# Hybrid RWKV-7 / latent-attention layer: eight places for the masked blocks of the recurrence, and raw weights in shared room

## The chip, the cores and the metric

One core of a Trainium2 chip. The core has TensorE (PE, matrix products; the profile shows its weight loads apart as PEld), VectorE (DVE), ScalarE (ACT), GpSimd (POOL) and SyncE (SP). Most transfers are issued from SP's queue, some from POOL's and ACT's; each of these queues is served in order. SBUF holds the working data (128 partitions), PSUM the results of TensorE. The metric is the device time of one execution in microseconds (us).

## The reference

One decoder layer on 2048 tokens of width 1024, in float32. Cut to what matters here:

```python
u = rmsnorm(h, g_pre); proj = u @ w_in           # one input projection for everything
# branch A, RWKV-7, 8 heads x 64: token shift, then per token and head
sa = S @ -kk_t
S  = S * w_t + sa (kk_t * a_t)^T + v_t k_t^T      # the state S is 64 x 64
y_t = S @ r_t                                    # then group norm, bonus, SiLU gate, w_out_a
# branch B: latent attention with rotary keys, SiLU gate, w_out_b
merged = sigmoid(gates_a) * y_a + sigmoid(gates_b) * y_b
h = h + rmsnorm(merged @ w_o, g_post)
```

## The kernel before

Products that need float32 accuracy are made from a high and a low part: `split` casts the high part on ACT and subtracts for the low part on POOL or DVE, and `mm3` makes three products per pair.

The kernel has three stages. The first holds the input projections, the elementwise work of branch A, the recurrence and the gate projections; the second is attention; the third is the output. The change touches the first stage, and names of room in the second.

**Projections.** `proj_seg(s)` works on one of four segments of 512 tokens. `make_xT` normalises the four tiles of x (ACT squares a tile into a scratch output `xjunk`, DVE scales it) and TensorE transposes them into X. Then 17 tiles of 128 columns are projected. `load_w` brings a tile's weights in two halves: a raw half (tag `wraw`, two places) is loaded and split into `whl` (three places); some split tiles are stored and later read back with no split. About half the tiles of segment 0 aren't stored, and are loaded raw again in segment 1. `shift` mixes each result with that of the token before: ACT's product `mf` (two places), DVE's sum in `fsh` (two places), which is then stored. At the start the two small raw weights of the low-rank projections (`lraw`) use the tag `fsh` too.

**The recurrence.** A half segment is 256 tokens, four chunks of 64; there are eight half segments (k = 0 to 7).
- `elem(k)` makes its decays and scaled keys (tiles AR, BK).
- `zblock(k, c)` makes the products of chunk c for all heads, masks them on DVE into a place of Zr, and stores the small diagonal blocks.
- `gather` reads those back, `invert` inverts 32 x 32 blocks with 60 small DVE steps, and `merge` joins them to 64 x 64 inverses.
- `chunk(k, c)` uses a place of Zr, the inverse and the state; it writes the next state (DVE, tile `uv`) and adds to the outputs Y in PSUM.
- `gnorm(k)` normalises the outputs: DVE reads Y's room through transposes `ypt`, which use the same PSUM banks as Y, adds the bonus that was stored in d_ya and stores the sum, four times, through `bvb` (two places).

Zr has six places: place (4k + c) mod 6. `step(k)` issues the chunks of half segment k - 1 among the blocks of half segment k, with `elem(k + 1)`:

```python
zblock(k, E, 0); zblock(k, E, 1)
chunk(k - 1, Ep, 0, ...);  zblock(k, E, 2)
chunk(k - 1, Ep, 1, ...);  zblock(k, E, 3);  gather(k, E)
chunk(k - 1, Ep, 2, ...);  chunk(k - 1, Ep, 3, ...)
# then invert(k), tokmaj(k), gnorm(k - 1), elem(k + 1) in turns, and merge(k)
```

**Order.** The program text gives priorities. A planner walks through it with a model of times, and each engine and queue takes the first instruction in the text that is ready in that model and has room for its tile. The order on each engine is fixed when the kernel is built. Some products (`pin`, `alternate`) keep the order of the text among themselves. Tiles with the same tag share its places; a new tile waits until one is given back.

Of the kernel before, what the change touches and what calls it, by code (L numbers as in the profile page):

```python
# [19 lines left out]
P = 128  # L20
# [29 lines left out]
def hybrid_layer(ctx, tc, x, positions, g_pre, w_in, b_gate, mu_shift, w0, w_decay_up, a0, w_iclr_up, k_k, k_a,  # L50
# [156 lines left out]
    def make_xT(pool, psp, ptag, pbufs, s, g_rep, Xs):  # L207

        XH, XL = Xs
        for i in range(4):  # L210
            tt = s * 4 + i
            if tt < len(x0):
                xt = x0[tt]
            else:
                xt = pool.tile([P, D], F32, name="xt", tag="xt", bufs=2)
                nc.sync.dma_start(xt, x[tt * P:(tt + 1) * P, :])
            junk = pool.tile([P, D], BF16, name="xjunk", tag="xjunk", bufs=1)
            ss = pool.tile([P, 1], F32, name="xss", tag="xss", bufs=2)
            rstd = pool.tile([P, 1], F32, name="xrs", tag="xrs", bufs=2)
            A.activation(junk, xt, AF.Square, accum_out=ss)  # L220
            if s:
                G.tensor_scalar(ss, ss, 1.0 / D, EPS, op0=ALU.mult, op1=ALU.add)
                G.tensor_tensor(rstd, ss, mhalf[:, 0:1], op=ALU.pow)
            else:
                V.tensor_scalar(ss, ss, 1.0 / D, EPS, op0=ALU.mult, op1=ALU.add)
                A.activation(ss, ss, AF.Sqrt)
                V.reciprocal(rstd, ss)
            V.scalar_tensor_tensor(xt, xt, rstd, g_rep, op0=ALU.mult, op1=ALU.mult)
            for k in range(2):
                pt = psp.tile([P, 512], F32, name="xps", tag=ptag, bufs=pbufs)  # L230
                for c in range(4):
                    PE.transpose(pt[:, c * P:(c + 1) * P], xt[:, (4 * k + c) * P:(4 * k + c + 1) * P], ident)
                pv = pt.rearrange("p (c t) -> p c t", c=4)
                hi = XH[:, 4 * k:4 * k + 4, i * P:(i + 1) * P]
                A.copy(hi, pv)
                V.tensor_tensor(XL[:, 4 * k:4 * k + 4, i * P:(i + 1) * P], pv, f32(hi), op=ALU.subtract)
        if s < NS - 1:
            for k in range(4):
                nc.sync.dma_start(d_x[s, k], f32(Xs[k // 2][:, k % 2 * 4:k % 2 * 4 + 4, :]))
# [10 lines left out]

    d_w = {}

    def load_w(pool, src, nk, n, elo=None, bufs=3, tag="w", pieces=None, raws=2, key=None, keep=True):


        res = []
        kept = d_w.get(key)
        if key is not None and kept is None and keep:
            d_w[key] = dtile(f"d_w{key}", [P, -(-nk // 4), 2, 4, n])
        for k0 in range(0, nk, 4):  # L260
            m = min(4, nk - k0)
            w = pool.tile([P, 2, m, P], F32R, name=f"{tag}hl", tag=f"{tag}hl", bufs=bufs)
            wn = w if n == P else w[:, :, :, 0:n]
            if kept is not None:
                nc.sync.dma_start(f32(wn), kept[:, k0 // 4])
            else:
                raw = pool.tile([P, m, P], F32, name=f"{tag}raw", tag=f"{tag}raw", bufs=raws)
                for lo_, n_, ap in (pieces or [(0, n, src)]):
                    nc.sync.dma_start(raw[:, :, lo_:lo_ + n_],
                                      ap[k0 * P:(k0 + m) * P, :].rearrange("(c p) n -> p c n", p=P))  # L270
                split(wn[:, 0], wn[:, 1], raw[:, :, 0:n], A, elo or G)
                if key is not None and keep:
                    nc.sync.dma_start(d_w[key][:, k0 // 4], f32(wn))
            res += [(w[:, 0, c, 0:n], w[:, 1, c, 0:n]) for c in range(m)]
        return res
# [26 lines left out]
    with st:  # L302
# [16 lines left out]
        Xinv = [sb.tile([P, 16, HD], F32, name=f"Xinv{i}") for i in range(2)]  # L319
        for i in range(2):  # L320
            G.memset(Xinv[i], 0.0)
        NZ = 6
        Zr = sb.tile([P, NZ, 2, NP, P], F32, name="Zr")

        def shift(ps, j):

# [6 lines left out]
            return f  # L333

        def wtile(c0, n=P, elo=None, keep=True):
            return load_w(sa, w_in[:, c0:c0 + n], KC, n, elo, key=f"i{c0}", keep=keep)

        def pj():
            return ppa.tile([P, 512], F32, name="pj", tag="pj", bufs=2)
# [89 lines left out]
        def proj_seg(s):  # L429
# [7 lines left out]
                return bool(s or i % 2)  # L437


            ps = pj()  # L440
            proj(ps, wtile(1536, elo=G if s else V, keep=later(0)), X, 2)
            f = shift(ps, 12)
# [17 lines left out]
            for p in range(NP):  # L460
                for nm, c0, j in (("r", 0, 0), ("v", 1024, 8)):
# [6 lines left out]
            ps = pj()  # L468
            k1 = w_in[:, C_KPE:C_KPE + 32]
            proj(ps[0:HD, :], load_w(sa, None, KC, HD, pieces=[(0, 32, k1), (32, 16, k1[:, 16:32]),  # L470
                                                               (48, 16, k1[:, 0:16])], key="kpe"), X)
            rt = sa.tile([P, 512], F32, name="rtab", tag="mf", bufs=2)
            nc.sync.dma_start(rt[0:HD], d_rope[32:96, cols_])
            ra = sa.tile([P, 512], F32, name="ra", tag="fsh", bufs=2)
# [10 lines left out]
        def gates_seg():  # L485

            xs = NS - 1
            for s, i in d_zg:
                if s != xs:
                    xs = s  # L490
                    load_xT(X, s)
                ps = pj()
                c0 = (C_ZA, C_ZB, C_G, C_G + 4 * P, C_G + 8 * P, C_G + 12 * P)[i // 4] + (i % 4) * P
                proj(ps, wtile(c0), X)
                th = sa.tile([P, 512], F32, name="thg", tag="mf", bufs=2)
                if i < 8:
                    A.activation(th, ps, AF.Tanh, scale=0.5)
                    V.scalar_tensor_tensor(th, th, 1.0, ps, op0=ALU.add, op1=ALU.mult)
                else:
                    A.activation(th, ps, AF.Tanh, scale=0.5, bias=dcol(HBG, i - 8))  # L500
                nc.sync.dma_start(d_zg[s, i], th)
                yield
# [4 lines left out]
        def elem(hs, E):  # L507
# [55 lines left out]
            def bonus(e2, p, rf):  # L563

                PE.matmul(e2, lhsT=blk1, rhs=rf, start=True, stop=True)

                def rest():
                    bv = se.tile([P, 256], F32, name="bv", tag="bv", bufs=2)
                    V.tensor_tensor(bv, e2, E["vf"][p], op=ALU.mult)
                    G.tensor_scalar(bv, bv, col("gb", p), None, op0=ALU.add)  # L570
                    nc.sync.dma_start(d_ya[p, s][:, cs_], bv)

                return rest
# [218 lines left out]
        def gnorm(hs, E):  # L792
# [18 lines left out]
                for p in range(NP):  # L811
                    PE.transpose(pts[p // 2][:, p % 2, i, :], y[:, p].rearrange("p h d -> p (h d)"), ident)
            for p in range(NP):
                bv = sb.tile([P, 256], F32, name="bvb", tag="bvb", bufs=2)
                nc.sync.dma_start(bv, d_ya[p, s][:, o:o + 256])
                V.scalar_tensor_tensor(bv, pts[p // 2][:, p % 2].rearrange("p i t -> p (i t)"), col("gg", p),
                                       bv, op0=ALU.mult, op1=ALU.add)
                nc.sync.dma_start(d_ya[p, s][:, o:o + 256], bv)
# [12 lines left out]
        def step(k):  # L831
# [3 lines left out]
                uvq[0] = uv_new() if k < NH else None  # L835
            el = elem(k + 1, new_E(k + 1)) if k + 1 < NH else iter(())
            if E:
                zblock(k, E, 0)
                zblock(k, E, 1)
            if Ep:  # L840
                chunk(k - 1, Ep, 0, Ep["uv"][1])
            if E:
                zblock(k, E, 2)
            yield
            if Ep:
                chunk(k - 1, Ep, 1, Ep["uv"][2])
            if E:
                zblock(k, E, 3)
                gather(k, E)
            next(el, None)  # L850
            yield
            if Ep:
# [20 lines left out]

        ropes = [rope_tables]
        run(proj_seg(0))
        run(elem(0, new_E(0)))
        for s in range(1, NS):
            for k in (0,) if s == 1 else (2 * s - 3, 2 * s - 2):
# [29 lines left out]
        wv3 = w_ukv.rearrange("k (h n) -> k h n", n=P)  # L908
        kws, qws = {}, {}

        def attn_weights(p, pool, bufs):

            kraw = pool.tile([P, 2, P], F32, name="kraw", tag="wqraw", bufs=1)[:, :, 0:HD]
            nc.sync.dma_start(kraw, wv3[:, 2 * p:2 * p + 2, 0:HD])
            kwh = pool.tile([P, P], F32R, name="kwh", tag="kwh", bufs=1)
            kwl = pool.tile([P, P], F32R, name="kwl", tag="kwl", bufs=1)
            split(kwh.rearrange("p (h n) -> p h n", h=2), kwl.rearrange("p (h n) -> p h n", h=2), kraw, A, V)

            kws[p], qws[p] = (kwh, kwl), []
            hq = [w_uq[:, (2 * p + h) * 96:(2 * p + h + 1) * 96] for h in range(2)]  # L920
            for pieces in ([(HD * h, HD, hq[h][:, 0:HD]) for h in range(2)],
                           [x for h in range(2) for x in ((32 * h, 32, hq[h][:, 64:96]),
                                                          (HD + 32 * h, 16, hq[h][:, 80:96]),
                                                          (HD + 32 * h + 16, 16, hq[h][:, 64:80]))]):
                qws[p].append(load_w(pool, None, 2, P, bufs=bufs, tag="wq", pieces=pieces, raws=1))

        tmp = sb.tile([P, NP, 4, P], F32R, name="vtmp", tag="AR", bufs=2).rearrange("p q c t -> p q (c t)")
        vh, vl = tmp[:, 0], tmp[:, 1]
# [1 line left out]
        nc.sync.dma_start(vraw.rearrange("p (h n) -> p h n", n=HD), wv3[:, :, HD:P])  # L930
        split(vh, vl, vraw, A, V)
        sw = kst.enter_context(tc.tile_pool(name="pw", bufs=1, reuse_waits="tile", side="right"))
        attn_weights(0, sw, 2)
        run(step(NH))

        def value(t):
# [62 lines left out]
        def queries(i, Q, sb, psp, ptag, pbufs, cqt=None, rt=None, mm=PE.matmul):  # L999

            p, g = divmod(i, NS)
            if g == 0:
                if p:
                    attn_weights(p, sb, 2)
                yield from keys(p, psp, ptag, pbufs, mm)
            if cqt is None:
                cqt = load_cq(g, sb)
# [419 lines left out]
```

## Time and profile before

| | us |
|---|---|
| median of 3 runs (lowest, highest) | 2454.78 (2450.98, 2462.46) |
| the profiled execution | 2459.4 |
| its span, first to last instruction | 2457.7 |
| TensorE busy in the span | 2216.5 |
| VectorE, ScalarE, GpSimd busy | 1099.8, 710.4, 1020.3 |

Busy time is the time in which at least one instruction of the engine ran. A row of a stretch has the start and the duration in us, the engine (SPq is SP's queue), the line, the operation, the tile written and those read, the shape, how many instructions of the kind stand in the row, and in brackets how long the engine had been idle before it and what ended that.

### The profile page before, as it was taken

What the parts mean: (1) busy time and instruction counts of PE and PEld (TensorE: products, weight loads), DVE (VectorE), ACT (ScalarE), POOL (GpSimd) and SP (SyncE); (2) the same over time, 40 slices, a digit from 0 to 9 for tenths busy, and PEclk for the clock granted to TensorE, in tenths of its full rate; (3) what the DMA queues carried; (4) which work ended last, traced back from release to release, by engine and by line L of the source; (5) the groups of instructions that cost most, each with busy time, mean ns of one, the idle gap of its engine ahead of it and who ended that gap; (6) DMA issues with size and microseconds to landing.
All of it is one profiled execution on the core that took longest, in us unless ns stands there. A gap on an engine that the chain in (4) does not pass through costs nothing.

```text
span 2457.7 us, 37858 instructions
## 1 busy us (share of the span) xinstructions
PE 2216.5 (90%) x14313; PEld 1646.5 (67%) x14313; DVE 1099.8 (45%) x2007; ACT 710.4 (29%) x1283; POOL 1020.3 (42%) x1194
## 2 busy tenths in 40 slices
PE   7978988988989897998698998988999989999997
PEld 5656776767766675776465655555678867788876
DVE  7155675667475847434353435344230231300312
ACT  4343342333324342123233333332321211111111
POOL 6474443445254655222245653555533232312422
PEclk9989989989999998999699999999999999999999
DMA  7777866647657787574211112050297895766863
GB/s 252 217 251 236 242 211 185 191 125 222 178 174 230 233 239 239 170 230 128 72 58 57 49 59 76 29 189 7 82 371 232 282 325 197 283 204 199 318 245 120
DMA packets 315182, 455.15 MB, mean 185 GB/s; under 512 B 114044, under 2 KB 207288, under 8 KB 309368
## 3 DMA queue, kind: packets, MB, share of 16 engines
q1 hardware_dynamic: 285112, 406.06, 51.3%
q0 software_dynamic: 12608, 42.47, 5.2%
q10 hardware_dynamic: 17280, 4.20, 1.0%
q8 instruction: 113, 1.85, 0.3%
q14 instruction: 69, 0.57, 0.1%
HBM read 313.69 MB, written 132.64 MB: 182 GB/s over the span
## 4 chain that ended last, share of the span: by engine, by line
PE 54%; DMA 18%; DVE 17%; POOL 3%; issue 3%; ACT 2%; SPq 2%; ACTq 0%; DVEq 0%; POOLq 0%
PE pj L281 7%; PE pst L294 7%; PE pj L282 7%; PE pj L283 7%; PE po L294 5%; DMA wraw<-in_w_in_dram 3%; DMA whl<-d_wi 3%; DVE mx L1049 3%; DMA Xg<-d_q 2%; DVE Xg L698 2%; DVE tq L696 2%; PE py L281 2%; PE py L283 2%; PE py L282 2%; PE pq L294 2%
## 5 line engine op out<-in xcount | busy, mean ns | idle before, releaser
L281 PE MATMUL pj<-xh,whl 128*128 128x512 f32 (+1 forms) x1320 | 536.4, 406 | 46.3 <-DMA whl<-d_wi 27.1
L283 PE MATMUL pj<-xh,whl 128*128 128x512 f32 (+1 forms) x1320 | 531.9, 403 | 10.0 <-POOL whl L248 9.7
L282 PE MATMUL pj<-xl,whl 128*128 128x512 f32 (+1 forms) x1320 | 529.9, 401 | 0.0
L1172 POOL TENSOR_TENSOR acc<-acc,pt 128x1024 f32<-128x1024 f32 (+2 forms) x144 | 290.5, 2017 | 204.7 <-PE po L294 177.4
L281 PEld LDWEIGHTS pj<-xh,whl 128*128 128x128 f32 x1320 | 256.2, 194 | 116.6 <-DMA whl<-d_wi 29.6
L283 PEld LDWEIGHTS pj<-xh,whl 128*128 128x128 f32 x1320 | 256.1, 194 | 74.1 <-POOL whl L248 15.3
L282 PEld LDWEIGHTS pj<-xl,whl 128*128 128x128 f32 x1320 | 256.4, 194 | 55.6 <-issue 2.5
L1049 DVE TENSOR_REDUCE mx<-pm 128x2 f32<-128x1024 f32 (+3 forms) x160 | 164.4, 1060 | 148.1 <-PE pm L294 147.4
L248 POOL TENSOR_TENSOR whl<-wraw,whl 128x512 fp32r<-128x512 f32 (+1 forms) x114 | 147.4, 1294 | 160.9 <-ACT whl L247 155.8
L1352 DVE SCALAR_TENSOR_TENSOR tg<-tg,py 128x512 f32<-128x512 f32 x64 | 43.9, 687 | 306.0 <-PE py L283 207.1
L1159 ACT ACTIVATE pt<-pst 128x1024 f32<-128x1024 f32 (+2 forms) x144 | 125.2, 883 | 163.5 <-PE pst L294 150.4
L1354 POOL TENSOR_TENSOR tg<-tg 128x512 f32<-128x512 f32 x32 | 41.2, 1288 | 211.7 <-DVE tg L1352 211.7
L247 ACT CAST whl<-wraw 128x512 fp32r<-128x512 f32 (+1 forms) x116 | 71.1, 615 | 179.4 <-DMA wraw<-in_w_in_dram 106.1
L294 PE MATMUL po<-pt,Vt 128*64 128x512 f32 (+3 forms) x576 | 121.4, 538 | 0.0
L281 PE MATMUL py<-BH,whl 128*128 128x512 f32 x256 | 103.2, 404 | 10.2 <-DMA whl<-d_wo 5.2
L294 PE MATMUL pm<-KH,QH 64*128 64x512 f32 (+3 forms) x312 | 71.6, 447 | 40.5 <-DVE mx L1049 34.8
L282 PE MATMUL py<-BL,whl 128*128 128x512 f32 x256 | 102.8, 402 | 0.0
L283 PE MATMUL py<-BH,whl 128*128 128x512 f32 x256 | 102.6, 402 | 0.0
L696 DVE TENSOR_TENSOR tq<-Xg,Qg 128x30 f32<-128x30 f32 (+7 forms) x240 | 84.8, 353 | 38.4 <-DMA Xg<-d_q 33.0
L282 PE MATMUL pout<-wf,MH 128*128 128x512 f32 x256 | 101.1, 395 | 0.0
L283 PE MATMUL pout<-wf,ML 128*128 128x512 f32 x256 | 99.5, 395 | 0.0
L281 PE MATMUL pout<-wf,MH 128*128 128x512 f32 x256 | 97.3, 395 | 0.1
(368 smaller groups left out, 3953.1 us busy)
## 6 DMA issues: line engine op xcount, KB each, us to landing
whl<-d_wi SPq DMA_DIRECT2D x222, 512.0 KB
d_wi<-whl SPq DMA_DIRECT2D x80, 512.0 KB
wraw<-in_w_in_dram SPq DMA_DIRECT2D x98, 256.0 KB
whl<-d_wo SPq DMA_DIRECT2D x48, 512.0 KB
wf<-d_wf SPq DMA_DIRECT2D x48, 512.0 KB
cqt<-d_cq POOLq DMA_DIRECT2D x16, 1024.0 KB, 5.5
d_zg<-thg SPq DMA_DIRECT2D x42, 256.0 KB
xl<-d_x POOLq DMA_DIRECT2D x8, 1024.0 KB, 9.9
```

The lines of the kernel that those rows point to most:

```text
L247: (ehi.copy if ehi is A else ehi.tensor_copy)(hi, src)
L248: elo.tensor_tensor(lo, src, f32(hi), op=ALU.subtract)
L281: mm(ps, lhsT=lh, rhs=rh, start=(i == 0), stop=False)
L282: mm(ps, lhsT=lh, rhs=rl, start=False, stop=False)
L283: mm(ps, lhsT=ll, rhs=rh, start=False, stop=(stop and i == n - 1))
L294: tc.keep_in_program_order(PE.matmul(*args, **kw))
L696: V.tensor_tensor(t3, Xg[:, 0:m, s_:s_ + 1].to_broadcast([P, m, n]), Qg[:, s_:s_ + 1, s_ + 1:32].to_broadcast([P, m, n]), op=ALU.mult)
L698: V.tensor_tensor(Xg[:, 0:m, s_ + 1:32], Xg[:, 0:m, s_ + 1:32], t3, op=ALU.add)
L1049: V.tensor_reduce(mx[:, :, j, c], pm[:, :, 0:w], axis=AX.X, op=ALU.max)
L1159: A.activation(pt[:, :, q0:512], pst[:, :, q0:512], AF.Exp, scale=scale)
L1172: G.tensor_tensor(acc[:, :, q0:512], acc[:, :, q0:512], pt[:, :, q0:512], op=ALU.add)
L1352: V.scalar_tensor_tensor(tg, tg, 1.0, po, op0=ALU.add, op1=ALU.mult)
```

## The change

Zr gets eight places, so that the blocks of two half segments fit; the four blocks of a half segment and its gather are issued ahead of the first chunk of the one before. In segment 0 the raw weights are loaded into the room that Zr takes afterwards (16 places); in the later segments they share `mf`, and in the gate projections `xt`. The scratch output of the Square shares `fsh`; `bv` and `bvb` have one place each; attention's raw weights share `bs`.

```diff
-            junk = pool.tile([P, D], BF16, name="xjunk", tag="xjunk", bufs=1)
+            junk = pool.tile([P, D], BF16, name="xjunk", tag="fsh", bufs=2)
...
-                raw = pool.tile([P, m, P], F32, name=f"{tag}raw", tag=f"{tag}raw", bufs=raws)
+                raw = raw_of(w) if raw_of else pool.tile([P, m, P], F32, name=f"{tag}raw", tag=f"{tag}raw", bufs=raws)
...
-        NZ = 6
-        Zr = sb.tile([P, NZ, 2, NP, P], F32, name="Zr")
+        NZ = 8
+        zraw = sb.tile([P, 4 * NZ // 2, 4, P], F32, name="zraw", tag="Zr", bufs=1)
+        nraw = [0]
+        def raw_first(w):
+            nraw[0] += 1
+            return zraw[:, nraw[0] % (4 * NZ // 2)]
+        def raw_gate(w):
+            return sa.tile([P, 2, 4, P], F32, name="graw", tag="xt", bufs=2)[:, 0]
+        def raw_here(w):
+            return sa.tile([P, 4, P], F32, name="wraw", tag="mf", bufs=2)
...
+            raw_of[0] = raw_here if s else raw_first
...
-                    bv = se.tile([P, 256], F32, name="bv", tag="bv", bufs=2)
+                    bv = se.tile([P, 256], F32, name="bv", tag="bv", bufs=1)
...
-                bv = sb.tile([P, 256], F32, name="bvb", tag="bvb", bufs=2)
+                bv = sb.tile([P, 256], F32, name="bvb", tag="bvb", bufs=1)
...
             if E:
-                zblock(k, E, 0)
-                zblock(k, E, 1)
+                for c in range(4):
+                    zblock(k, E, c)
+                gather(k, E)
             if Ep:
                 chunk(k - 1, Ep, 0, Ep["uv"][1])
-            if E:
-                zblock(k, E, 2)
             yield
             if Ep:
                 chunk(k - 1, Ep, 1, Ep["uv"][2])
-            if E:
-                zblock(k, E, 3)
-                gather(k, E)
...
         run(proj_seg(0))
+        Zr = sb.tile([P, NZ, 2, NP, P], F32, name="Zr", tag="Zr", bufs=1)
         run(elem(0, new_E(0)))
...
+            def raw_of(w):
+                return rpool.tile([P, 2, P], F32, name="wqraw", tag="bs", bufs=1)
...
-                qws[p].append(load_w(pool, None, 2, P, bufs=bufs, tag="wq", pieces=pieces, raws=1))
+                qws[p].append(load_w(pool, None, 2, P, bufs=bufs, tag="wq", pieces=pieces, raw_of=raw_of))
```

## Rows read from the trace of the kernel before

**Rows 1.** The page: busy us (share of the span) xinstructions of each engine.
```profile
PE 2216.5 (90%) x14313; PEld 1646.5 (67%) x14313; DVE 1099.8 (45%) x2007; ACT 710.4 (29%) x1283; POOL 1020.3 (42%) x1194
```

**Rows 2.** Busy time by stretch: from:to and length, engines, granted clock, DMA share, GB/s.
```profile
0.00:1150.00 1150.00, 1017.26 (x7679) 778.45 (x7680) 680.50 (x1472) 398.66 (x809) 524.28 (x828) 0.94 0.69 208
1150.00:1200.00 50.00, 24.29 (x135) 17.89 (x134) 15.68 (x24) 7.19 (x14) 9.62 (x28) 0.66 0.43 121
```

**Rows 3.** Waits of TensorE, 0 to 1150: waiter, releaser, total us, times, longest.
```profile
PE pj L281 <- DMA whl<-d_wi: 21.0, 12, 5.8
PE pj L283 <- POOL whl L248: 9.7, 7, 4.8
...
PE Y L299 <- DVE bvb L816: 4.3, 1, 4.3
PE Y L294 <- DVE bvb L816: 4.2, 3, 2.4
...
PE pz L299 <- DVE uv L686: 2.5, 1, 2.5
```

**Rows 4.** VectorE in order of time, 632 to 670: half segment 4.
```profile
640.13 1.29 DVE L644 TENSOR_TENSOR Zr<-pz,mask 128x512 f32<-128x512 f32 x2 [1.63 <-PE pz L294]
...
647.15 1.29 DVE L644 TENSOR_TENSOR Zr<-pz,mask 128x512 f32<-128x512 f32 x2
648.35 0.85 DVE L780 TENSOR_TENSOR uv<-ch,sp 64x256 f32<-64x256 f32 x2
...
654.64 1.29 DVE L644 TENSOR_TENSOR Zr<-pz,mask 128x512 f32<-128x512 f32 x2 [0.33 <-PE pz L294]
...
665.15 0.88 DVE L780 TENSOR_TENSOR uv<-ch,sp 64x256 f32<-64x256 f32 x2 [2.35 <-PE ch L776]
666.05 1.29 DVE L644 TENSOR_TENSOR Zr<-pz,mask 128x512 f32<-128x512 f32 x2
```

**Rows 5.** All engines in order of time, the start of the program.
```profile
4.43 1.06 ACT L220 ACTIVATE xjunk<-x 128x1024 bf16<-128x1024 f32 x1 [2.35 <-DMA x<-in_x_dram]
...
8.79 0.45 PE L232 MATMUL xps<-ident,x 128*128 128x128 f32 x1 [8.79 <-POOL selw L130]
...
18.37 1.44 POOL L313 TENSOR_TENSOR wd<-lraw,wd 64x512 fp32r<-64x512 f32 x1
...
22.62 0.58 PE L281 MATMUL pj<-xh,whl 128*128 128x256 f32 x1 [0.74 <-DVE xl L236]
```

**Rows 6.** TensorE in order of time: first and last of seven stops in segment 0.
```profile
37.93 0.50 PE L281 MATMUL pj<-xh,whl 128*128 128x512 f32 x1 [1.73 <-ACT whl L247]
...
105.91 0.50 PE L283 MATMUL pj<-xh,whl 128*128 128x512 f32 x1 [0.64 <-POOL whl L248]
```

**Rows 7.** The page's costliest groups: busy us, mean ns of one, idle before, releaser.
```profile
L248 POOL TENSOR_TENSOR whl<-wraw,whl 128x512 fp32r<-128x512 f32 (+1 forms) x114 | 147.4, 1294 | 160.9 <-ACT whl L247 155.8
```

**Rows 8.** ScalarE in order of time: the Square of a tile of segment 3.
```profile
343.34 1.06 ACT L220 ACTIVATE xjunk<-xt 128x1024 bf16<-128x1024 f32 x1 [1.61 <-DMA xt<-in_x_dram]
```

**Rows 9.** All engines in order of time, 1151 to 1184: the way into attention.
```profile
1151.36 0.87 DVE L816 SCALAR_TENSOR_TENSOR bvb<-ypt,prm,bvb 128x256 f32<-128x256 f32 x2
...
1152.26 0.96 PE L294 MATMUL pv<-vtmp,kvl 128*128 128x512 f32 x3
...
1156.76 0.79 SPq L815 DMA_DIRECT2D bvb<-d_ya  x2
1159.05 0.88 DVE L816 SCALAR_TENSOR_TENSOR bvb<-ypt,prm,bvb 128x256 f32<-128x256 f32 x2 [4.70 <-DMA bvb<-d_ya]
...
1160.76 2.31 SPq L974 DMA_DIRECT2D KR<-d_kr  x2
...
1183.07 1.01 PE L294 MATMUL pn<-identr,mh 128*1 128x128 f32 x8 [20.18 <-DVE QL L248]
```

**Rows 10.** Waits of SP's queue, 0 to 1200, and waits before `bvb`'s instructions.
```profile
SPq L815 <- DMA d_ya<-bvb: 29.3, 15, 5.0
...
  DMA bvb<-d_ya: 13.3, 4
```

More of the change, by code (lines that the diff above doesn't have):

```diff
@@ L251, in hybrid_layer, with load_w @@
     d_w = {}
-    def load_w(pool, src, nk, n, elo=None, bufs=3, tag="w", pieces=None, raws=2, key=None, keep=True):
+    def load_w(pool, src, nk, n, elo=None, bufs=3, tag="w", pieces=None, raws=2, key=None, keep=True, raw_of=None):
         res = []
@@ L321, in hybrid_layer @@
             G.memset(Xinv[i], 0.0)
-        NZ = 6
-        Zr = sb.tile([P, NZ, 2, NP, P], F32, name="Zr")
+        NZ = 8
[8 more added lines that the diff above has]
+            return sa.tile([P, 4, P], F32, name="wraw", tag="mf", bufs=2)
+        raw_of = [raw_first]
         def shift(ps, j):
@@ L335, in wtile @@
         def wtile(c0, n=P, elo=None, keep=True):
-            return load_w(sa, w_in[:, c0:c0 + n], KC, n, elo, key=f"i{c0}", keep=keep)
+            return load_w(sa, w_in[:, c0:c0 + n], KC, n, elo, key=f"i{c0}", keep=keep, raw_of=raw_of[0])
         def pj():
@@ L470, in proj_seg @@
             proj(ps[0:HD, :], load_w(sa, None, KC, HD, pieces=[(0, 32, k1), (32, 16, k1[:, 16:32]),
-                                                               (48, 16, k1[:, 0:16])], key="kpe"), X)
+                                                               (48, 16, k1[:, 0:16])], key="kpe", raw_of=raw_of[0]), X)
             rt = sa.tile([P, 512], F32, name="rtab", tag="mf", bufs=2)
@@ L487, in gates_seg @@
             xs = NS - 1
+            raw_of[0] = raw_gate
             for s, i in d_zg:
@@ L909, in hybrid_layer, with attn_weights @@
         kws, qws = {}, {}
-        def attn_weights(p, pool, bufs):
-            kraw = pool.tile([P, 2, P], F32, name="kraw", tag="wqraw", bufs=1)[:, :, 0:HD]
+        def attn_weights(p, pool, bufs, rpool):
+            kwh = pool.tile([P, 2, HD], F32R, name="kwh", tag="kwh", bufs=1)
+            kwl = pool.tile([P, 2, HD], F32R, name="kwl", tag="kwl", bufs=1)
+            def raw_of(w):
+                return rpool.tile([P, 2, P], F32, name="wqraw", tag="bs", bufs=1)
+            kraw = raw_of(None)[:, :, 0:HD]
             nc.sync.dma_start(kraw, wv3[:, 2 * p:2 * p + 2, 0:HD])
-            kwh = pool.tile([P, P], F32R, name="kwh", tag="kwh", bufs=1)
-            kwl = pool.tile([P, P], F32R, name="kwl", tag="kwl", bufs=1)
-            split(kwh.rearrange("p (h n) -> p h n", h=2), kwl.rearrange("p (h n) -> p h n", h=2), kraw, A, V)
+            split(kwh, kwl, kraw, A, V)
+            kwh, kwl = (t.rearrange("p h n -> p (h n)") for t in (kwh, kwl))
             kws[p], qws[p] = (kwh, kwl), []
@@ L932, in hybrid_layer @@
         sw = kst.enter_context(tc.tile_pool(name="pw", bufs=1, reuse_waits="tile", side="right"))
-        attn_weights(0, sw, 2)
+        attn_weights(0, sw, 2, sb)
         run(step(NH))
@@ L1003, in queries @@
                 if p:
-                    attn_weights(p, sb, 2)
+                    attn_weights(p, sb, 2, sb)
                 yield from keys(p, psp, ptag, pbufs, mm)
```

## Prediction
> **What bounds the kernel now.** I read the stage table first, then the waits of TensorE, then single stretches in order of time. TensorE is busy for 90% of the span [rows 1], so the question is which of its idle time the change can reach. The change touches the first stage, 0 to about 1150 us. There TensorE is busy for 1017.26 of 1150 us and its mean granted clock is 0.94 [rows 2]: 132.7 us of idle time, and about 0.06 x 1150 = 69 us lost because the clock stood at its lower level (1.2 instead of 2.4 GHz) for part of the stage. So nearly always a projection is there to fill TensorE; the recurrence is threaded into it.
>
> The waits of TensorE in this stage [rows 3] are many and short. The largest is for stored weights (21.0 us in 12 waits), then the splitting of raw weights by POOL (9.7). What hangs on the recurrence is small: 4.3 and 4.2 us where the state's output product (Y) waits for the group norm to give back its PSUM, 2.5 us where a masked product waits for PSUM.
>
> **What the eight places do.** With six places, the third masked block of a half segment waits until the first chunk of the half segment before has read its place, the fourth until the second chunk. Half segment 4 shows it [rows 4]: block one is multiplied by the mask at 640.13, block three at 654.64, right behind the state update that ended at 649.2; the next update ends at 666.03 and block four follows at 666.05. The blocks are some 7 us apart where nothing holds them (640.13, 647.15), so alone they would be done at about 661: 5 us sooner. Then come the gather, the inversion and the merge, so the recurrence can gain about 5 us in each of seven half segments, 35 us in all. But this is time of the recurrence, not of TensorE: as long as projections fill TensorE, its total in the stage is the same, and the gain moves filler to the end. On TensorE's own path I count only the stop that the block products show, 2.5 us (bounds: 0, and C below for all of it): **-2.5**.
>
> **What the room costs.** The two more places take 8 KB of each partition, and the rest of the diff pays for them.
>
> *The start.* The Square's scratch output now comes from the two "fsh" places. At the start both hold the small raw weights of the decay and ICLR projections, allocated ahead of it in the program. POOL gives the first back when L313 ends, at 18.37 + 1.44 = 19.81 [rows 5]. The first Square ran at 4.43 and the first projection matmul at 22.62, 18.2 us later; 0.7 of that waited for x, which will then long be there. So the first projection comes at about 19.81 + 17.5 = 37.3: +14.7 if POOL keeps its order, 0 if the planner finds a place sooner. POOL was busy without a pause, so I take **+14**.
>
> *Raw weights of the first segment.* They get 16 places in the room that becomes the masked blocks, so loads run far ahead of use. Seven stops of TensorE between 37.93 and 105.91, 8.2 us in all (1.73 + 0.64 + 1.07 + 0.64 + 2.42 + 1.05 + 0.64; first and last in [rows 6]), wait for a raw tile's split. With the raw tiles there early I let them all go: **-8** (bounds 0 and -8). What is late next is POOL's half of the split, two of 1.29 us per projection [rows 7] against 24 matmuls on TensorE, which leaves room.
>
> *Raw weights of the second segment* share two places with the shift's product ("mf"). Nine projections have raw weights; at worst each evacuation waits for one more split of 1.29 us [rows 7]: 0 to 11.6. Two PSUM banks cover most of it: **+2**. The gates' raw weights take the two x places, as many as before and empty by then: 0. Attention's raw weights move to "bs", again one place: 0, under the gate projections.
>
> *Squares ahead of their segment.* At 343.34, in the middle of segment 2, ACT squares a tile of segment 3 [rows 8]. This now needs a free "fsh" place between two stores. If none is free until the segment ends, the transposes come one Square-to-transpose chain later, 4.4 us (4.43 to 8.79 [rows 5]), at three boundaries: 0 to 13. A Square is 1.06 us and slips in easily: **+2**.
>
> *One result buffer instead of two in the group norm* ("bvb": load, add, store, four times per half segment). Now two loads are made ahead, and the other two wait for a store to land. The last half segment shows the cycle [rows 9]: results at 1151.36, refill issued at 1156.76, results at 1159.05: 7.7 us. With one buffer three refills per half segment wait, not one round of them. Today this holds SP's queue for 29.3 us in 15 waits and DVE for 13.3 us [rows 10], and TensorE stops for 8.5 us at Y. Behind the waiting load on SP stand weight loads and the stores that feed the inversion; behind the waiting add on DVE stand the inversion's steps and the state updates. Three rounds for one make 2 x 8.5 = 17 us more of TensorE's stops at most, 0 if the planner moves other work in front. It knows of the wait but places it too early by about the waits seen, so I take a quarter: **+4**. "bv", also single now, has a whole pair's work (some 10 us) between uses: 0.
>
> The Trainium skill (DMA: Bandwidth & Descriptors, section on the anatomy of one DMA) gives a DMA about 2.0 us plus its bytes over 436 GB/s. For 128 KB out and back with the add that makes an estimate of 5.1 us for the cycle, and the term would be a third smaller. The trace says 7.7, and the measurement decides.
>
> *The way into attention.* TensorE stops for 20.18 us before 1183.07 [rows 9]: the rotary keys' loads begin at 1160.76, behind the last "bvb" work on SP, though the value products, whose room they seem to take, ended at 1153.2. If the recurrence ends sooner, these loads begin up to 7.6 us earlier; if two more cycles stand before them, 15.4 us later. I take **-5**, as the planner sees that loads with free room can go first.
>
> **The sum.** -2.5 + 14 - 8 + 2 + 2 + 4 - 5 = +6.5 us. The profiled execution took 2459.4 us (span 2457.7 plus 1.7 around it), 4.6 above the median of 2454.78; so 2465.9 for such an execution and **2461** for a median.
>
> **Rivals.**
>
> A, the forecast: TensorE stays the bound, and the freed recurrence buys nothing but its end; small losses of the room decide. 2461, by itself from 2449 to 2473. For it: 90% busy and filler to the end. Chance 0.42.
>
> B, slower: the single result buffer becomes the wait that replaces the one removed. All 17 us of stops come, and each us of stop costs 69 / 132.7 = 0.52 us more in lower clock: 17 x 1.52 = 26 instead of 4, so 2483; with the keys' loads held behind the longer last group norm, up to 2503. For it: SP and DVE run in order, and DVE already waits there. Against it: the planner sees the buffer and can put other work first. It decides when the stops at Y for "bvb" exceed some 16 us. The Trainium skill (Trainium Kernel Development and Optimization, Best Practices) tells one to double-buffer so that DMA and compute overlap; by that rule this is the outcome, and the 13.3 us that DVE waits there even with two buffers agree. Chance 0.30.
>
> C, faster: the 35 us by which the recurrence ends sooner empty the way into attention. The window 1150 to 1200 has 25.7 us idle and a clock of 0.66 [rows 2], 17 us more. If the last chunks and group norm are over before the value products, about 20 us of that go, and the loss in B stays away: 2461 - 4 - 20 = 2437. For it: the last group norm's results come at 1159.05 [rows 9], after all filler. Against it: the keys' loads need room that the value products hold until 1153. Chance 0.25. That the blocks never waited for the state is nearly excluded by rows 4; it would be A with 2 us more. Others 0.03.
>
> **How the numbers follow.** 0.5% is 12.3 us, about what a measurement of this kernel tells from no change. A gives mostly "same" (0.33), some slower (0.06) and faster (0.03); B slower 0.27, same 0.03; C faster 0.25. With the rest spread: faster 0.29, same 0.37, slower 0.34. The range 2425 to 2495 takes in most of C and of B; A's own is 2449 to 2473.
>
> **What would show it.** Right: the first Square at about 20 us and the first projection near 37; no stop for a raw split in the first segment; blocks three and four of each half segment 7 us apart, free of the state update; DVE's wait for "bvb" grown to two or three times 13.3 us; the last group norm's results well before 1159. Wrong: a first Square near 4 us; stops at Y for "bvb" above 16 us (B); the stop before attention gone (C); or TensorE's busy time in the first 1150 us below 1000, which would mean that the recurrence, not TensorE, had been the bound.

## The result and the profile after

The changed kernel takes 2471.41 us (median of 6 runs, 2467.34 to 2479.24), the kernel before 2454.15 in the same comparison: ratio 1.007, 95% interval 1.0045 to 1.0094, slower by 0.7%. The profiled execution has a span of 2468.2 us against 2457.7, 10.5 more; that is less than the 17.3 between the medians, as the one before lies 5 us above its median and this one 1.5 below. These are the answers to [rows 1, 2]: the page's busy time, then the two stretches (from:to and length, busy us of PE, PEld, DVE, ACT and POOL, granted clock, DMA share, GB/s).

```profile
PE 2211.8 (90%) x14313; PEld 1642.4 (67%) x14313; DVE 1098.9 (45%) x2007; ACT 713.0 (29%) x1283; POOL 1014.9 (41%) x1194
```

```profile
0.00:1150.00 1150.00, 1001.03 (x7616) 764.97 (x7617) 673.69 (x1454) 395.05 (x798) 521.81 (x839) 0.95 0.70 208
1150.00:1200.00 50.00, 25.46 (x123) 18.44 (x122) 20.32 (x37) 10.19 (x21) 4.26 (x14) 0.74 0.41 124
```

TensorE has the same 14313 matmuls. By 1150 us it has done 16 us less of them (1001.03 for 1017.26), with 63 matmuls fewer; the granted clock of the stretch hardly moved (0.95 for 0.94).

The start came as forecast. All engines in order of time, the answers to [rows 5]:

```profile
17.56 1.25 POOL L313 TENSOR_TENSOR wd<-lraw,wd 64x512 fp32r<-64x512 f32 x1
18.85 1.06 ACT L220 ACTIVATE xjunk<-x 128x1024 bf16<-128x1024 f32 x1 [2.59 <-POOL wd L313]
...
24.36 1.94 PE L232 MATMUL xps<-ident,x 128*128 128x128 f32 x8 [24.36 <-POOL selw L135]
...
35.40 0.38 PE L281 MATMUL pj<-xh,whl 128*128 128x256 f32 x1 [0.74 <-DVE xl L236]
```

The bracket of the Square names its releaser: POOL's last reading of `lraw` (17.56 + 1.25 = 18.81), 0.04 us before. The first projection is 35.40 - 22.62 = 12.8 us late.

The blocks are free of the state, the answer to [rows 4]; VectorE, half segment 4:

```profile
639.04 1.29 DVE L660 TENSOR_TENSOR Zr<-pz,mask 128x512 f32<-128x512 f32 x2 [2.68 <-PE pz L294]
646.28 1.29 DVE L660 TENSOR_TENSOR Zr<-pz,mask 128x512 f32<-128x512 f32 x2 [5.95 <-PE pz L294]
647.49 0.85 DVE L796 TENSOR_TENSOR uv<-ch,sp 64x256 f32<-64x256 f32 x2
653.77 1.29 DVE L660 TENSOR_TENSOR Zr<-pz,mask 128x512 f32<-128x512 f32 x2 [5.44 <-PE pz L294]
660.69 1.29 DVE L660 TENSOR_TENSOR Zr<-pz,mask 128x512 f32<-128x512 f32 x2 [5.62 <-PE pz L294]
667.68 0.87 DVE L796 TENSOR_TENSOR uv<-ch,sp 64x256 f32<-64x256 f32 x2 [1.85 <-PE ch L792]
```

Block four now comes 7 us ahead of the second state update; before it came right behind it, 5.4 us later than here.

TensorE's waits from 0 to 1150 (waiter, releaser, total us, times, longest; beside [rows 3]):

```profile
...
PE rn L618 <- ACT ta L603: 19.1, 10, 3.4
PE pj L281 <- DMA whl<-d_wi: 18.5, 12, 3.3
PE wa L599 <- DVE bv L585: 11.5, 7, 2.5
...
PE pj L281 <- DVE fsh L345: 6.0, 4, 2.1
...
PE pj L283 <- POOL whl L248: 3.2, 4, 1.9
```

Beside the start, two waits inside `elem` grew most: for PSUM that ACT's `ta` reads (`rn`, 19.1 us) and that `bv` reads (`wa`, 11.5). Before, they were:

```profile
...
PE wa L583 <- DVE bv L569: 6.5, 3, 3.8
...
PE rn L602 <- ACT ta L587: 5.2, 5, 2.2
```

In segment 0 alone (22 to 155 us), the stops for evacuations and split raw weights are now:

```profile
...
PE pj L281 <- DVE fsh L345: 6.0, 4, 2.1
PE pj L281 <- ACT whl L247: 4.7, 2, 3.9
...
PE pj L283 <- POOL whl L248: 0.2, 1, 0.2
```

The stops at Y for `bvb` (8.5 us) are gone altogether. The wait for `bvb` itself grew on SP's queue (29.3 us before) and on VectorE (13.3), in the answers to [rows 10]:

```profile
SPq L831 <- DMA d_ya<-bvb: 35.6, 23, 8.6
```

```profile
DVE bvb L832 <- DMA bvb<-d_ya: 33.8, 16, 5.6
```

The Squares no longer run ahead. Before, the second of segment 3 ran at 343.34 [rows 8] and the first at 337.77; now the first waits for the last reader of `fsh` in segment 2:

```profile
539.83 1.06 ACT L220 ACTIVATE xjunk<-xt 128x1024 bf16<-128x1024 f32 x1 [0.29 <-POOL ra L493]
```

And the way into attention, all engines in order of time, the answers to [rows 9]:

```profile
1151.56 0.47 DVE L832 SCALAR_TENSOR_TENSOR bvb<-ypt,prm,bvb 128x256 f32<-128x256 f32 x1
...
1156.06 0.48 DVE L832 SCALAR_TENSOR_TENSOR bvb<-ypt,prm,bvb 128x256 f32<-128x256 f32 x1 [0.25 <-DMA bvb<-d_ya]
...
1161.32 0.48 DVE L832 SCALAR_TENSOR_TENSOR bvb<-ypt,prm,bvb 128x256 f32<-128x256 f32 x1 [1.88 <-DMA bvb<-d_ya]
...
1165.77 0.48 DVE L832 SCALAR_TENSOR_TENSOR bvb<-ypt,prm,bvb 128x256 f32<-128x256 f32 x1 [3.97 <-DMA bvb<-d_ya]
...
1174.58 0.97 PE L294 MATMUL pv<-vtmp,kvl 128*128 128x512 f32 x3
1175.58 1.71 SPq L992 DMA_DIRECT2D KR<-d_kr  x4
...
1189.36 0.84 SPq L1007 DMA_DIRECT2D rt<-d_rope  x2
...
1192.91 0.68 DVE L1033 TENSOR_TENSOR qra<-pq,rt 64x512 f32<-64x512 f32 x1 [11.92 <-DMA rt<-d_rope]
...
1197.49 1.01 PE L294 MATMUL pn<-identr,mh 128*1 128x128 f32 x8 [15.76 <-DVE QL L248]
```

Three things are to be seen. The four results come one by one, some 4.5 to 5.3 us apart, and the last ends 6.3 us later than before (1166.25 for 1159.93). The keys' loads (the 24 of the full tables `KR`; six for a smaller table of the first queries are issued earlier) start not there but when the last value product ends (1174.58 + 0.97 = 1175.55), 14.8 us later than before. And `pn` hangs on them: the load of the query table `rt` stands behind the 24 in SP's queue, VectorE's `qra` waits for it (14.28 us before), and `pn` comes behind `QL`, 14.4 us late. From the keys' loads to the end of the span it is 1292.6 us here and 1296.9 before: the whole loss lies ahead of that point. TensorE's work up to the end of the value products is the same in both (1020.48 and 1019.62 us busy), so what was added there is idle time.

### The profile page after: what moved, and what is told of

Its sections match the earlier page's. It is cut to its first block, busy times and chain, and to the rows that moved or that the text cites. A ratio compares the mean times of both kernels' runs of the same rounds, so it can differ in the third digit from the quotient of the medians.

```text
span 2468.2 us, 37822 instructions
## 1 busy us (share of the span) xinstructions
PE 2211.8 (90%) x14313; PEld 1642.4 (67%) x14313; DVE 1098.9 (45%) x2007; ACT 713.0 (29%) x1283; POOL 1014.9 (41%) x1194
## 4 chain that ended last, share of the span: by engine, by line
PE 57%; DVE 19%; DMA 13%; issue 4%; POOL 3%; ACT 2%; SPq 1%; ACTq 0%; DVEq 0%; POOLq 0%
PE pj L281 7%; PE pj L283 7%; PE pj L282 7%; PE pst L294 7%; PE po L294 5%; DVE mx L1067 3%; DVE Xg L714 2%; DVE tq L712 2%; DMA whl<-d_wi 2%; PE pout L281 2%; PE pout L282 2%; PE pout L283 2%; PE pm L294 2%; PE py L281 2%; PE py L282 2%
## 5 line engine op out<-in xcount | busy, mean ns | idle before, releaser
L281 PE MATMUL py<-BH,whl 128*128 128x512 f32 x256 | 103.8, 406 | 11.6 <-DVE tg L1370 11.4
L712 DVE TENSOR_TENSOR tq<-Xg,Qg 128x30 f32<-128x30 f32 (+7 forms) x240 | 77.0, 321 | 39.8 <-DMA Xg<-d_q 34.2
L782 POOL TENSOR_TENSOR sp<-uv,pcs 64x256 f32<-64x256 f32 x64 | 41.4, 647 | 119.8 <-DVE uv L796 112.2
L294 PEld LDWEIGHTS pm<-KH,QH 64*128 64x128 f32 x312 | 32.1, 193 | 82.9 <-DVE mx L1067 53.1
```

The costliest lines, as they stand in the source:

```text
L281: mm(ps, lhsT=lh, rhs=rh, start=(i == 0), stop=False)
L294: tc.keep_in_program_order(PE.matmul(*args, **kw))
L712: V.tensor_tensor(t3, Xg[:, 0:m, s_:s_ + 1].to_broadcast([P, m, n]), Qg[:, s_:s_ + 1, s_ + 1:32].to_broadcast([P, m, n]), op=ALU.mult)
L782: G.tensor_tensor(sp[b], uv[b, h], pcs[b, c, :].unsqueeze(2).to_broadcast([HD, NP, HD]), op=ALU.mult)
```

## The experiments

Every kernel below was timed against the kernel before (2454 to 2456 us in each comparison). The theory at first was that the Square's scratch in `fsh` costs nearly everything (S); rivals were the single result buffer (B), the raw weights (R) and the order (O).

**e1_lraw**, the changed kernel with:
```diff
-            raw = sa.tile([P, 512], F32, name="lraw", tag="fsh", bufs=2)
+            raw = zraw[:, 15 if lora else 0].rearrange("p c t -> p (c t)")
```
(the raw room is allocated ahead of it for that).

> The changed kernel, with the two small raw weights (lraw) of the start moved from the fsh places to the raw room, so that the first Square finds a free place. Theory S (the Square's scratch in fsh is what costs): first Square back near 4.4 us and first projection matmul from 35.4 to about 23 us; these 12 to 13 us stay in the total, 2459 to 2462, while the Squares of the later segments still wait for the end of the segment before. Rival R (raw weights and their splits bound segment 0, so an earlier start is given back): first projection near 23 us, but total 2468 to 2473. Rival B (the single result buffer costs): total unchanged, 2468 to 2473.

Measured 2467.63, ratio 1.0056 (1.0033 to 1.0080). The first projection is back at 23.88, but only 3.8 us of the 11.5 stay, and the two intervals overlap. S fails here; R and B named 2468 to 2473, nearly this.

**e2_junk**, the kernel before with one line of the change:
```diff
-            junk = pool.tile([P, D], BF16, name="xjunk", tag="xjunk", bufs=1)
+            junk = pool.tile([P, D], BF16, name="xjunk", tag="fsh", bufs=2)
```


> The kernel before, with the Square's scratch in fsh and nothing else changed. Theory S: first projection matmul from 22.6 to 35 us or later, Squares of segments 1 to 3 only at the end of the segment before, total 13 to 20 us above the kernel before: 2467 to 2474. Rival R: the late start is given back behind the raw weights: 2454 to 2460. Rival B: 2454 to 2460.

Measured 2491.84, ratio 1.0151 (1.0123 to 1.0179): 38 us slower, over twice the loss of the whole change. All three expectations miss. So the rest of the change takes back some 20 us of what this line costs by itself; which part of it does is open. The first projection is at 35.04, the first Square of segment 3 at 529.33, and the way into attention ends with the value products:

```profile
1191.27 0.97 PE L294 MATMUL pv<-vtmp,kvl 128*128 128x512 f32 x3
...
1192.27 1.72 SPq L974 DMA_DIRECT2D KR<-d_kr  x4
```

**e3_bv1**, the kernel before with one place each:
```diff
-                    bv = se.tile([P, 256], F32, name="bv", tag="bv", bufs=2)
+                    bv = se.tile([P, 256], F32, name="bv", tag="bv", bufs=1)
...
-                bv = sb.tile([P, 256], F32, name="bvb", tag="bvb", bufs=2)
+                bv = sb.tile([P, 256], F32, name="bvb", tag="bvb", bufs=1)
```


> The kernel before, with one place instead of two for bvb and for bv, nothing else changed. Theory S: VectorE and SP wait longer for bvb (30 us and more), but TensorE's stops at Y for bvb stay under 10 us and the total within 4 us of before: 2450 to 2458. Rival B: stops at Y above 16 us, total 2466 to 2475.

Measured 2457.18, ratio 1.0010 (0.9992 to 1.0027): no change by the timing, and stops at Y for `bvb` of 7.5 us (6.7 and 0.8). S named 2450 to 2458, and B, as the prediction had it, is out. But the trace shows the same single cycles in the last group norm, and the keys' loads behind them, 15.4 us later than before:

```profile
1174.93 0.48 DVE L816 SCALAR_TENSOR_TENSOR bvb<-ypt,prm,bvb 128x256 f32<-128x256 f32 x1 [4.02 <-DMA bvb<-d_ya]
...
1176.17 1.71 SPq L974 DMA_DIRECT2D KR<-d_kr  x4
```

This profiled execution (2467.35) is the slowest of the kernel's 12, so its trace shows the mechanism but overstates the median.

**e5_ownjunk**, the changed kernel with:
```diff
-            junk = pool.tile([P, D], BF16, name="xjunk", tag="fsh", bufs=2)
+            junk = se.tile([P, D], BF16, name="xjunk", tag="xjunk", bufs=1)
```
(the two one-column tiles beside it are joined to one to make room).

> The changed kernel, with a place of its own for the Square's scratch again; all other edits of the change stay. Theory S: start as in the kernel before (first Square near 4.4, first projection near 22.6 us), Squares ahead of their segments again, total 14 to 20 us below the changed kernel: 2451 to 2457. Rival O (the order of the steps and the shared raw rooms cost the rest): only the start comes back, 2458 to 2463. Rival B: 2465 to 2473.

Measured 2466.04, ratio 1.0047 (1.0030 to 1.0064): S falls, O (2458 to 2463) misses too, and B's 2465 to 2473 holds, though at another place than Y. TensorE's work by 1150 us is back at 1014.62 us, the value products end at 1156.11; and still the keys' loads wait:

```profile
1155.15 0.96 PE L294 MATMUL pv<-vtmp,kvl 128*128 128x512 f32 x3
...
1175.62 0.48 DVE L832 SCALAR_TENSOR_TENSOR bvb<-ypt,prm,bvb 128x256 f32<-128x256 f32 x1 [6.56 <-DMA bvb<-d_ya]
1176.55 1.96 SPq L992 DMA_DIRECT2D KR<-d_kr  x4
...
1196.22 1.01 PE L294 MATMUL pn<-identr,mh 128*1 128x128 f32 x8 [16.62 <-DVE QL L248]
```

So a second theory (K): the keys' loads start at the later of two ends, that of the value products, which the scratch delays, and that of the last group norm result, which the single buffer delays. The next edit gives all four results a place, in room of other steps whose tags they share:

```diff
-                bv = sb.tile([P, 256], F32, name="bvb", tag="bvb", bufs=1)
+                bv = sb.tile([P, 256], F32, name="bvb", tag=("bvb", "rs", "sp", "XT")[p], bufs=1)
```

**e6_four** is e5_ownjunk with this edit, **e7_after_four** the changed kernel with it, **e8_before_four** the kernel before with it, and **e9_four_old** e6_four with blocks three and four again behind the chunks (`zblock(k, E, 2)` after chunk 0; `zblock(k, E, 3)` and `gather` after chunk 1).

> The changed kernel with a place of its own for the Square's scratch (as in e5_ownjunk), and the group norm's four results in four places (bvb, and rs, sp and XT, which are idle then), so that all four loads are made ahead. Theory K (the way into attention: the loads of the rotary keys wait for the last group norm result, and with one place that comes three load-add-store cycles late, 1176.1 against 1159.5 us): the keys' loads start at 1156 to 1160 instead of 1176.6, the stop before the first pn goes back by some 15 us, total 2448 to 2454. Rival V (the value products' room holds the keys' loads anyway): 2460 to 2466.

> The changed kernel with four places for the group norm's results and nothing else; the Square's scratch stays in fsh. Theory K with the start's loss: in the changed kernel the value products end at 1175.5 and the keys' loads start at 1175.6, while the last group norm result is at 1166; so four places move nothing, 2467 to 2474. Rival B (the cycles of the single result buffer cost the 17 us themselves): 2454 to 2461.

> The kernel before with four places for the group norm's results (bvb, rs, sp, XT) and nothing else. Theory K: last result at 1152 instead of 1159, keys' loads behind the value products at about 1153.5 instead of 1160.8, total 2445 to 2449. Rival V: 2452 to 2457.

> e6_four with the old order of the steps (blocks three and four behind the chunks of the half segment before), still eight places and shared raw rooms. Theory A (TensorE is the bound, the freed recurrence buys nothing): within 5 us of e6_four. Rival C (the decoupled order shortens the recurrence and with it the stage): 8 us or more slower than e6_four.

Measured: e6_four 2444.33, ratio 0.9960 (0.9944 to 0.9975); e7_after_four 2477.27, 1.0100 (1.0080 to 1.0120); e8_before_four 2442.65, 0.9950 (0.9934 to 0.9966); e9_four_old 2444.85, 0.9964 (0.9948 to 0.9980). Each rival named with them fails; e6 and e8 came out 2 to 4 us below what K expected, and e7 3 us above. The way into attention, first of e6_four, then of e7_after_four:

```profile
1140.97 0.87 DVE L832 SCALAR_TENSOR_TENSOR bvb<-ypt,prm,bvb 128x256 f32<-128x256 f32 x2
...
1143.93 0.97 PE L294 MATMUL pv<-vtmp,kvl 128*128 128x512 f32 x3
1144.93 1.71 SPq L992 DMA_DIRECT2D KR<-d_kr  x4
...
1165.64 1.01 PE L294 MATMUL pn<-identr,mh 128*1 128x128 f32 x8 [14.55 <-DVE QL L248]
```

```profile
1163.11 1.66 DVE L832 SCALAR_TENSOR_TENSOR bvb<-ypt,prm,bvb 128x256 f32<-128x256 f32 x4
...
1180.47 0.97 PE L294 MATMUL pv<-vtmp,kvl 128*128 128x512 f32 x3
1181.47 1.72 SPq L992 DMA_DIRECT2D KR<-d_kr  x4
```

Four of these kernels make a square. Medians in us (from three comparisons, in which the kernel before differs by 2 us):

| | scratch in `fsh` | scratch in its own place |
|---|---|---|
| one result place | 2471.41 (the change) | 2466.04 (e5_ownjunk) |
| four result places | 2477.27 (e7_after_four) | 2444.33 (e6_four) |

Its own place for the scratch alone gives 5 us, with overlapping intervals; four result places alone lose 6; both together give 27. That is the mark of two waits that end at one point. And e9_four_old equals e6_four: with both losses mended, the order that the eight places allow is worth nothing that can be measured. It does not even end the recurrence sooner: the last group norm result ends at 1141.84 in e6_four and at 1131.55 in e9_four_old.

**e10_lraw_four** (e1_lraw with the four places: only the segments' boundaries keep the shared scratch) and **e11_start_four** (e6_four, with the scratch in `fsh` in segment 0 only) split the scratch's loss.

> The changed kernel with four places for the results and the small raw weights of the start out of fsh (as in e1_lraw): the start is that of the kernel before, but the Squares of segments 1 to 3 still wait for fsh until the segment before ends. With the result buffer out of the way the shared scratch cost 33 us (e7_after_four against e6_four). Theory P (it is mostly the segments' boundaries: 18 to 22 of the 33): 2460 to 2468. Rival T (it is mostly the start): 2443 to 2452.

> e6_four with the Square's scratch in fsh in segment 0 alone, where lraw holds it; in the other segments it has its own place. Theory P: only the start's 12 to 13 us are lost, 2454 to 2460. Rival T: 2468 to 2478. Rival R (the late start is given back behind later waits): 2442 to 2449.

Measured 2448.02, ratio 0.9972 (0.9960 to 0.9985), and 2458.09, ratio 1.0013 (0.9998 to 1.0027). Against e6_four's median the boundaries alone cost 4 us, the start alone 14, both 33 (e7_after_four). The first lies in T's range, the second in P's: P had the start right and the boundaries wrong (4, which is not clear of the spread, for 18 to 22). By the ends of the value products (1144.90 in e6_four, 1161.37, 1169.33, and 1181.44 with both) it is 16.5, 24.4 and 36.5. The profiled executions themselves (2438.97, 2452.29, 2462.35 and 2472.70) give 13, 23 and 34 us, which nearly add up; but e6_four's lies 5 us below its median and e10_lraw_four's 4 above. Why the medians don't add up is open.

**e12_two_queues**, e8_before_four with half of the keys' loads on POOL's queue:
```diff
-                    nc.sync.dma_start(f32(K4[32 * r:32 * r + 32, ss_]), f32(d_kr[:, 0, ss_]))
+                    (G if r % 2 else nc.sync).dma_start(f32(K4[32 * r:32 * r + 32, ss_]), f32(d_kr[:, 0, ss_]))
...
-                    nc.sync.dma_start(f32(K5[HD * h:HD * h + 32, ss_]), f32(d_kr[:, 1, ss_]))
+                    (G if h else nc.sync).dma_start(f32(K5[HD * h:HD * h + 32, ss_]), f32(d_kr[:, 1, ss_]))
```


> e8_before_four with half of the rotary keys' loads issued from POOL's queue instead of SP's. In e8_before_four the query table's load (rt) stands behind 24 of them, 13.5 us after the first. Theory K: rt is loaded some 6 us sooner, the first pn 5 to 6 us sooner, total 2434 to 2440. Rival M (the transfers themselves, not their issue, take the time): 2441 to 2446.

Measured 2446.51, ratio 0.9970 (0.9956 to 0.9985): no gain over e8_before_four; K misses, and M (2441 to 2446) just. The table `rt` did come sooner (issued at 1158.21 for 1164.52), but `cqt`, on POOL's queue, now stands behind the keys' loads (in e8_before_four it was issued at 1125.88, ahead of them), and the query product waits for it:

```profile
1152.99 1.10 POOL L974 DMA_DIRECT2D KR<-d_kr  x2 [26.76 <-PE pv L294]
...
1160.08 0.56 POOL L984 DMA_DIRECT2D cqt<-d_cq  x1 [0.15 <-issue]
...
1167.11 4.55 PE L294 MATMUL pq<-cqt,wqhl 128*128 128x512 f32 x12 [14.41 <-DMA cqt<-d_cq]
```

The first row also names what the keys' loads wait for, on an engine that had been idle for 26.76 us: PE's last value product. How the last result holds them is not separated: in the traces where it ends last, its store stands right ahead of them in SP's queue, and their room may also wait for it.

**e13_two**, e5_ownjunk with two result places, tags ("bvb", "rs")[p % 2].

> e5_ownjunk with two places for the group norm's results (bvb and rs) instead of one. Theory K: one refill round instead of three in the last half segment, the last result some 11 us sooner, and less waiting at VectorE and SP before: 2451 to 2458, about the kernel before. Rival V: 2462 to 2468.

Measured 2432.88, ratio 0.9913 (0.9890 to 0.9935): faster than both kernels and than every other tried here, 18 us below what K expected, and 29 below V. Its way into attention:

```profile
1136.96 0.96 PE L294 MATMUL pv<-vtmp,kvl 128*128 128x512 f32 x3
...
1140.13 0.47 DVE L832 SCALAR_TENSOR_TENSOR bvb<-ypt,prm,bvb 128x256 f32<-128x256 f32 x1
...
1141.04 1.78 SPq L992 DMA_DIRECT2D KR<-d_kr  x4
...
1161.51 1.01 PE L294 MATMUL pn<-identr,mh 128*1 128x128 f32 x8 [16.36 <-DVE QL L248]
```

In all fourteen traces the keys' loads start within 0.9 us behind the later of the two ends. Worked out from the rows (us):

| kernel | value products end | last result ends | keys' loads start | span less that |
|---|---|---|---|---|
| before | 1153.22 | 1159.93 | 1160.76 | 1296.9 |
| the change | 1175.55 | 1166.25 | 1175.58 | 1292.6 |
| e2_junk | 1192.24 | 1175.51 | 1192.27 | 1293.7 |
| e5_ownjunk | 1156.11 | 1176.10 | 1176.55 | 1290.2 |
| e6_four | 1144.90 | 1141.84 | 1144.93 | 1292.4 |
| e7_after_four | 1181.44 | 1164.77 | 1181.47 | 1289.5 |
| e13_two | 1137.92 | 1140.60 | 1141.04 | 1288.7 |

The last column lies between 1288.7 and 1296.9 in all fourteen, so the start of these loads, which moves by 51 us, tells the span to within 8 us.

## Why the prediction was right or wrong

The time lies in the range and in A's own range (2449 to 2473), 10 us above the 2461 forecast; what was held likeliest, no measurable change, did not come out, but a loss of 0.7%. The sum can be followed through the profiled pair (us, change less before):

| | forecast | measured |
|---|---|---|
| to the end of the value products | -2.5 + 14 - 8 + 2 + 2 + 4 = +11.5 | 1175.55 - 1153.22 = +22.3 |
| from there to the keys' loads | -5 | 0.03 - 7.54 = -7.5 |
| from the loads to the end | 0 | -4.3 |
| span | +6.5 | +10.5 |

So the miss lies in the first line, and the two below it hide part of it: that the time fell within A's range is in part luck. e5_ownjunk divides the first line: from the kernel before to e5_ownjunk, all but the scratch, it is +2.9 where the terms make -4.5; from there to the change, the scratch, it is +19.4 where they make +16. Step by step:

- **-2.5, the block products' stop**: gone, but by luck. [rows 3] name `uv` L686 as its releaser, the copy of the transposed values in `tokmaj`, which held PSUM; the state is written in L780, and eight places of Zr don't touch that stop. The reading of [rows 4] holds for block four alone: it came 11.4 us after block three, which itself came 7.5 after block two, as it does in the change. That the freed recurrence buys nothing by itself (rival A) holds where it was tested (e9_four_old against e6_four).
- **+14, the start**: right in place and size, 12.8 us. That it stays to the end, where the group norm does not hide it, is shown by e11_start_four with 14.
- **-8, the stops for split raw weights in segment 0**: failed. These stops went from 8.2 only to 4.9 us (4.7 for ACT's cast, 0.2 for POOL), and the 6.0 us of stops for the evacuation (`pj` on `fsh`) all stand in segment 0: 10.9 in all. "With the raw tiles there early I let them all go" left out what is late next.
- **+2, raws in `mf`**, and 0 for `bv`: not tested by themselves. e6_four and e9_four_old hold all of the change but the scratch and the single buffer `bvb`, and stand 2 us above e8_before_four, within the measurement; so -2.5, -8, +2 and 0 come to about nothing together, not to -8.5. In the change the stop at `wa` for `bv` grew by 5.0 us, and that at `rn`, of which the sum has nothing, by 13.9.
- **+2, Squares ahead of their segment**: too small. That a Square "slips in easily" is wrong: the trace has it only behind the last reader of `fsh`. It costs 4 us alone, not clear of the spread, and 19 on top of the late start (2477.27 - 2458.09).
- **+4, one result buffer**: in the place that was argued (stops at Y) it cost nothing in the change, and B's mechanism did not come: 0 us of stops where it needed 16, and at most 7.5 (e3_bv1) in the other kernels with one place. What TensorE did in their stead no row shows. The cost is real, but it sits in the next step. The estimate of 5.1 us for a cycle, from the Trainium skill (DMA: Bandwidth & Descriptors, anatomy of one DMA), uses a fit that the section gives for transfers issued by GpSimd, while these go out on SP's queue. Single cycles took 4.4 to 7.0 us in the change and in e5_ownjunk.
- **-5, the way into attention**: near in size, -7.5 at the loads and a stop before `pn` of 15.76 us for 20.18, but not for its reason. The last result did not come sooner but 6.3 us later. The value products, 22.3 us late, ended last and hid the group norm's cycles behind them. Where they are in time, the other end that the prediction named came true: "if two more cycles stand before them, 15.4 us later", and e3_bv1 and e5_ownjunk show 15.4 and 15.8. The size is partly luck: in e5_ownjunk three cycles take 18.4 us for one of 7.7, and the first result is 5.9 us later besides. That "loads with free room can go first" did not hold there: the value products end at 1156.11 in e5_ownjunk, and the loads still wait for the last result.

Rival C's time was reached, though not by its mechanism: without the two losses the same change, with two result places, takes 2432.88, below C's 2437, but its last results end behind the value products (1140.60 and 1137.92) and TensorE still stops for 16.36 us before `pn`. How much of that is the new order is open: e9_four_old says nothing of it in the plan with four places, and there is no twin of e13_two in the old order. Open too is why two places beat four by 11 us (one lead: with four, `merge` waits 11.1 us for the group norm's stores, as `XT` shares a place with a result; e13_two has no such wait), why a single place costs the kernel before only 3 us and e5_ownjunk 33 against e13_two, and why a stop for `fsh` appeared in segment 0: it goes with the late start under the whole change's edits (6.0 us here, 4.4 in e7_after_four, 2.8 in e11_start_four; at most 1.0 where the start is early), but e2_junk, as late, has none. Each edit of room makes the planner write a new order for the whole stage, so differences of some 10 us between plans that no row explains are not to be read as the price of the edit.

## What to carry to other kernels

When room is taken from small buffers to pay for a large one, look at each of them at the ends of a stage, not at its mean: the scratch output of the first instruction and the result buffer of the last group norm cost most there. Where two chains end at one point, mending one can show little; try the pair before calling either harmless. When the reason for a gain is "the planner can put it earlier", first find in the trace what its room or its queue waits for.

## What the runs showed of the hardware

In e12_two_queues the place of a transfer in its queue mattered more than the cost of issuing it. Twelve loads moved from SP's queue to POOL's took some 0.5 us each to issue there, for 0.42 on SP. But `cqt` behind them was issued 7.4 us after the value products' end (1160.08 for 1152.70), and the query product began 7.0 us after that: TensorE stood for 14.41 us, and the 6.3 us that `rt` had gained on SP's queue were lost.
